# Encoder layer on one core: per-partition vectors by one transpose, one bias table of full width, one mask store per head and row half

## The chip, the cores and the metric

The kernel runs on one core of a Trainium2 chip. The metric is the device time of one execution in microseconds (us), lower is better. Times are medians over several executions; the profile is one execution, recorded by the hardware profiler, with times counted from the start of its span.

## The reference

One encoder layer is applied to two batches of 1024 tokens of width 1024, with the same weights, in f32. Cut to what matters here:

```
proj = x @ w_in                       # q, k, v of mixer A and B, and two gates
ya = mixer_a(...)                     # dilated sliding windows
# mixer B: 2-D neighbourhood attention, 8 heads, with a learned bias
bias = rpb[:, dr, dc]                 # rpb is (8 heads, 15, 31)
bias = where(ok, bias, -1e30)
scores = q k^T / 8 + bias
merged = sigmoid(ga + b_gate[0]) * ya + sigmoid(gb + b_gate[1]) * yb
x = layer_norm(alpha * x + merged @ w_out, ln1_g, ln1_b)
hid = square(relu(x @ w_ff1 + b_ff1))
x = layer_norm(alpha * x + hid @ w_ff2 + b_ff2, ln2_g, ln2_b)
```

The vectors `b_gate`, `ln1_g`, `ln1_b`, `b_ff1` (called `b1`) and `b_ff2` (`b2`) are used per feature. Where features lie on partitions, each is wanted as a column: entry k*128 + p on partition p.

## The kernel before

`encoder_kernel` handles the two batches one after the other (loop over `b`). f32 products are made of three reduced-precision products of high and low parts (`mm3`, lines 107 to 109), so every operand is split: ScalarE (ACT) casts the high part, VectorE (DVE) or GpSimd (POOL) subtracts it to get the low part (line 103 is the helper `sub` for all such subtractions).

**Start of a batch.** Eight tiles of x (`xt`, line 298) are loaded and transposed on TensorE into `xT`. Then comes the V stage: three groups of V columns, of 384, 384 and 512 columns. For each group `load_v` loads eight row blocks of weights into the ring `wvr` (tile name "wvr" of the pool `vrp`, four buffers, line 291), ACT casts and POOL subtracts them into `wv`. For each of eight token tiles TensorE makes 24 matmuls into a PSUM tile `psv` (four buffers); ACT casts it into `vt` (two buffers, line 342), DVE subtracts the low part, and ACT's own DMA queue stores `vt` into the DRAM tensor `vd` (line 344). 192 matmuls make a group. After the V stage come the first projections of mixer A (`pmm`, two PSUM buffers, 24 matmuls each), read by ACT on line 451 (`r`), shuffled by DVE and multiplied on POOL (lines 453 and 454) by the rotary table `rope`, which is loaded into memory that the V stage gives back (line 355).

**Tables, in the first batch only.** `bias_tables` (from line 139) pads the learned bias to `rp`, stores it to DRAM (`prd`, line 147) and copies it DRAM to DRAM into three tables `ud`, one for each of three column types of width 24, 32 and 24 (line 153): 184 x 16 rows each, so that the bias of a query row is read as one long run. Then the vectors are loaded as columns: `bg`, `gb1`, `agb`, `b1t` (lines 311 to 320), every element an address of its own, and two combined vectors go back to DRAM as `agd` the same way (line 319). `mask_tables` (from line 156) makes, for each type, head and row half (3 x 8 x 2 = 48 units), the masked bias: load `bt` from `ud` (line 168, six buffers), add the mask `maskb` on POOL (line 171), store to `bmd` (line 172). Mixer B reads `bmd` much later (line 654).

**What sets the order.** The tile framework schedules the program: within an engine the instructions stand in a fixed order, found when the program is built. Loads and table stores stand in SP's queue in one order with the weights; `vd` stores stand in ACT's. A DMA signals its landing on one of eight counters, DMAHW0 to DMAHW7, which SP's and ACT's DMAs share: a DMA that is given a counter waits, in its queue, until the DMA before it on this counter has landed.

Of the kernel before, what the change touches and what calls it, by code (L numbers as in the profile page):

```python
# [9 lines left out]
F32 = mybir.dt.float32  # L10
F32R = mybir.dt.float32r
AF = mybir.ActivationFunctionType
ALU = mybir.AluOpType
# [5 lines left out]
P = 128  # L19
T = 1024  # L20
D = 1024
KT = D // P
FF = 4096
ALPHA = 2.0 ** 0.25
# [7 lines left out]
TYPE_W = (24, 32, 24)  # L32
TYPE_DC = (23, 15, 15)
NROW = 12
MOFF = (0, 288, 672, 960, 1248, 1632)
# [46 lines left out]
def encoder_kernel(ctx, tc, xs, w_in, b_gate, w_a, w_b, w_out, rpb, ln1_g, ln1_b, w1, b1, w2, b2,  # L82
# [3 lines left out]
    def pool(name, bufs=1, side=None, space=None):  # L86
        kw = {} if space is None else {"space": space}
        if space is not DRAM:
            kw["reuse_waits"] = "tile"
        if side is not None:  # L90
            kw["side"] = side
        return tc.alloc_tile_pool(name=name, bufs=bufs, **kw)
# [19 lines left out]
    const = ctx.enter_context(tc.tile_pool(name="const", bufs=1))  # L112
    ident = const.tile([P, P], F32, name="ident")
    nc.sync.dma_start(ident, ident_d)
    bg = const.tile([P, 2, KT], F32, name="bg")
    gb1 = const.tile([P, 2, KT], F32, name="gb1")
    b1t = const.tile([P, FF // P], F32, name="b1t")
    mhalf = const.tile([P, 1], F32, name="mhalf")
    nc.gpsimd.memset(mhalf, -0.5)
    lnc = const.tile([P, 3], F32, name="lnc")  # L120
# [11 lines left out]
    agd = dram.tile([2, D], F32, name="agd")  # L132
    rawd = [dram.tile([4, P, 2, 4, P], F32, name=f"rawd{b}") for b in range(len(xs))]
    prd = dram.tile([8, PR, PC], F32, name="prd")
    ud = [dram.tile([16, 8 * PR, TYPE_W[ty]], F32, name=f"ud{ty}") for ty in range(3)]

    bmd = [dram.tile([8, 2, P, NROW * TYPE_W[ty]], F32, name=f"bmd{ty}") for ty in range(3)]

    def bias_tables():

        bp = pool("biasprep", side="right")
        rp = bp.tile([8, PR, PC], F32, name="rp")
        nc.gpsimd.memset(rp, 0.0)
        rq = bp.tile([8, 15, 31], F32, name="rq")
        nc.sync.dma_start(rq, rpb)
        nc.gpsimd.tensor_copy(rp[:, 4:19, 8:39], rq)
        nc.sync.dma_start(prd, rp)
        bp.release()
        prh = prd[:]
        for ty in range(3):  # L150
            w = TYPE_W[ty]
            src = bass.AP(tensor=prh.tensor, offset=prh.offset + TYPE_DC[ty], ap=[[PC, 8 * PR], [-1, 16], [1, w]])
            nc.sync.dma_start(ud[ty].rearrange("q r c -> r q c"), src)

    def mask_tables():

        mbp = pool("maskb", side="right")
        maskb = mbp.tile([P, 1920], F32, name="maskb")
        nc.sync.dma_start(maskb, maskb_d)
        btp = pool("btm", 6, side="right")  # L160
        for ty in range(3):
            w = TYPE_W[ty]
            n = NROW * w
            u = ud[ty][:]
            for h in range(8):
                for rh in range(2):
                    t = btp.tile([P, 384], F32, name="bt", tag="bt")
                    nc.sync.dma_start(t[:, :n], bass.AP(tensor=u.tensor, offset=u.offset + (h * PR + 4 - 4 * rh) * w,
                                                        ap=[[w, 8], [8 * PR * w, 16], [1, n]]))
                    mo = MOFF[3 * rh + ty]  # L170
                    nc.gpsimd.tensor_tensor(t[:, :n], t[:, :n], maskb[:, mo:mo + n], op=ALU.add)
                    nc.sync.dma_start(bmd[ty][h, rh], t[:, :n])
        btp.release()
        mbp.release()

# [91 lines left out]
    for b, x in enumerate(xs):  # L267
# [40 lines left out]
        if b == 0:  # L308
            with tc.issue_after(ins.ins):
                bias_tables()  # L310
                nc.sync.dma_start(bg, b_gate.rearrange("s (k p) -> p s k", p=P))
                for i, v in enumerate((ln1_g, ln1_b)):
                    nc.sync.dma_start(gb1[:, i], v.rearrange("(k p) -> p k", p=P))
                agb = const.tile([P, 3, KT], F32, name="agb")
                nc.sync.dma_start(agb[:, 2], b2.rearrange("(k p) -> p k", p=P))
                nc.vector.tensor_scalar(agb[:, 0], gb1[:, 0], ALPHA, None, op0=ALU.mult)
                nc.vector.tensor_scalar(agb[:, 1], gb1[:, 1], ALPHA, None, op0=ALU.mult)
                nc.vector.tensor_tensor(agb[:, 1], agb[:, 1], agb[:, 2], op=ALU.add)
                nc.sync.dma_start(agd.rearrange("s (k p) -> p s k", p=P), agb[:, :2])
                nc.sync.dma_start(b1t, b1.rearrange("(k p) -> p k", p=P))  # L320
        vz = vtp.tile([64, 256], F32, name="vz", tag="vt")
        nc.gpsimd.memset(vz, 0.0)
        for q in range(2):
# [288 lines left out]
        for hp in range(4):  # L612
# [19 lines left out]
            for c2 in range(2):  # L632
# [8 lines left out]
                for hd in range(2):  # L641
                    d0 = slice(64 * hd, 64 * hd + 64)
                    po = pspo.tile([P, 2, 2, P], F32, name="po", tag="po")
                    for ci in range(2):
                        cb = 2 * c2 + ci
                        ty = CB_TYPE[cb]
                        w, c0 = TYPE_W[ty], CB_C0[cb]
                        n, kn = NROW * w, 4 * w
                        pth = pp.tile([P, 4, 2, P], F32R, name="pth", tag="pth")
                        ptl = pp.tile([P, 4, 2, P], F32R, name="ptl", tag="ptl")  # L650
                        for rh in range(2):
                            if (ty, hd, rh) not in bt:
                                t = btp.tile([P, 384], F32, name="bt", tag="bt")
                                nc.sync.dma_start(t[:, :n], bmd[ty][2 * hp + hd, rh])
                                bt[ty, hd, rh] = t
                            S = pss.tile([P, 384], F32, name="S", tag="S")
                            us = slice(512 * rh + P * cb, 512 * rh + P * (cb + 1))
                            Sv = S[:, :n].rearrange("p (r c) -> p r c", c=w)
                            kv_ = [t[:, 4 * rh:4 * rh + NROW, c0:c0 + w] for t in kv]
                            nc.tensor.matmul(Sv, qs[hd][:, us], kv_[hd], start=True, stop=False)  # L660
                            nc.tensor.matmul(Sv, qs[hd][:, us], kv_[2 + hd], start=False, stop=True)
                            st2 = sm.tile([P, 2], F32, name="st2", tag="st2")
                            pr = head_unit(S, n, bt[ty, hd, rh], (st2[:, 0:1], st2[:, 1:2]), True, 0, n)
                            pt = pspt.tile([P, 3, P], F32, name="pt", tag="pt")
# [449 lines left out]
```

## Time and profile before

| | before |
|---|---|
| median of 3 runs | 3175.51 us (3169.77 to 3178.15) |
| profiled execution | 3184.45 us |
| its span | 3182.6 us |
| TensorE (PE) busy | 2951.2 us, 93% |
| VectorE / ScalarE / GpSimd busy | 1881.0 / 1449.7 / 979.1 us |
| mean granted TensorE clock | 0.959 of full speed |

The span leaves out 1.85 us of the profiled execution. A window row gives, for a stretch of the span, each engine's busy us and number of instructions, the granted TensorE clock (1.00 is full speed, 2.4 GHz; 0.50 is 1.2 GHz; between them lies a mixture), the mean busy share of the 16 DMA engines and their rate. A timeline row gives the start, the duration, the engine and the instruction, and in brackets how long the engine had been idle before it and what ended that. "SPq" and "ACTq" rows are DMA issues; their duration is that of the issue, not of the transfer.

### The profile page before, as it was taken

Reading aid. Unit: us, or ns where it says so; the run is one execution under the profiler, and the core shown is the slowest. Engines: PE = TensorE matmul, PEld = TensorE weight load, DVE = VectorE, ACT = ScalarE, POOL = GpSimd, SP = SyncE. Lnnn points to the kernel's source line nnn. Section 1 sums busy time; section 2 is a strip of 40 time slices with the busy share of each in tenths; the row PEclk is TensorE's granted clock in tenths of the full one; section 3 lists DMA queues with packets and bytes.
Section 4 is the critical chain, followed back from the end, with each engine's and each line's share of the span. In section 5 each row is a group of like instructions: output and inputs, shape, how many; then the busy total and the mean of one; then the engine's idle time right before and its main releaser. Section 6 shows DMA issues by size and latency. Waiting matters only on the chain. (4 is left out here: it accounts for less than half of the span.)

```text
span 3182.6 us, 39432 instructions
## 1 busy us (share of the span) xinstructions
PE 2951.2 (93%) x13964; PEld 2441.7 (77%) x13964; DVE 1881.0 (59%) x3439; ACT 1449.7 (46%) x2640; POOL 979.1 (31%) x716
## 2 busy tenths in 40 slices
PE   7879898999997899899989998989999979998997
PEld 7757786888786788688878786878877767886886
DVE  1036566673465666687861565567444756558887
ACT  3136564554363455333441564646542735553333
POOL 3464563223203200133341655432130131004322
PEclk9989898999998999899999999989999989999998
DMA  8742224345546644654354123244454575466442
GB/s 182 255 130 81 74 71 119 119 131 189 174 143 189 201 159 159 237 177 155 96 195 141 56 79 90 66 135 121 158 157 151 169 226 191 146 210 208 148 139 86
DMA packets 404414, 470.22 MB, mean 148 GB/s; under 512 B 44841, under 2 KB 282225, under 8 KB 403961
## 3 DMA queue, kind: packets, MB, share of 16 engines
q1 hardware_dynamic: 377720, 429.43, 43.1%
q10 hardware_dynamic: 26496, 38.28, 3.6%
q8 instruction: 110, 1.80, 0.2%
q14 instruction: 88, 0.71, 0.1%
HBM read 326.77 MB, written 141.79 MB: 147 GB/s over the span
## 5 line engine op out<-in xcount | busy, mean ns | idle before, releaser
L107 PE MATMUL pmm<-bh,whi 128*128 128x512 f32 x1152 | 465.4, 404 | 29.5 <-ACT r L451 23.6
L108 PE MATMUL pmm<-bh,wlo 128*128 128x512 f32 x1152 | 463.2, 402 | 0.0
L109 PE MATMUL pmm<-bl,whi 128*128 128x512 f32 x1152 | 462.7, 402 | 0.0
L103 POOL TENSOR_TENSOR wlo<-wraw,whi 128x512 fp32r<-128x512 f32 (+1 forms) x176 | 231.8, 1331 | 533.0 <-ACT whi L195 493.1
L107 PEld LDWEIGHTS pmm<-bh,whi 128*128 128x128 f32 x1152 | 221.1, 192 | 72.8 <-ACT r L451 24.9
L109 PEld LDWEIGHTS pmm<-bl,whi 128*128 128x128 f32 x1152 | 220.9, 192 | 42.7
L108 PEld LDWEIGHTS pmm<-bh,wlo 128*128 128x128 f32 x1152 | 221.0, 192 | 40.3
L103 POOL TENSOR_TENSOR ts<-rw,rw 128x1024 f32<-128x1024 f32 x14 | 41.4, 2957 | 655.7 <-DMA rw<-in_w_ff_dram 497.4
L746 ACT CAST bh<-hr 128x1024 fp32r<-128x1024 f32 x56 | 58.7, 1048 | 366.0 <-PE px L109 216.9
L391 ACT ACTIVATE smk<-smk,nm 128x256 f32<-128x256 f32 (+4 forms) x320 | 162.0, 508 | 129.1 <-DVE nm L390 126.1
L103 DVE TENSOR_TENSOR ptl<-pt,pth 128x512 fp32r<-128x512 f32 (+3 forms) x224 | 125.3, 569 | 67.4 <-ACT pth L667 36.7
L107 PE MATMUL psv<-wv,bh 128*128 128x384 f32 (+1 forms) x384 | 139.7, 365 | 19.8 <-DVE vt L103 18.2
L103 DVE TENSOR_TENSOR vt<-psv,vt 128x384 fp32r<-128x384 f32 (+1 forms) x48 | 28.8, 602 | 214.4 <-ACT vt L342 214.4
L108 PE MATMUL psv<-wv,bl 128*128 128x384 f32 (+1 forms) x384 | 139.9, 364 | 0.3 <-DVE bl L103 0.3
L109 PE MATMUL psv<-wv,bh 128*128 128x384 f32 (+1 forms) x384 | 138.5, 363 | 1.6 <-POOL wv L103 1.5
L107 PE MATMUL px<-bh,oh 128*128 128x512 f32 x256 | 106.4, 416 | 32.4 <-ACT oh L746 25.3
L103 POOL TENSOR_TENSOR qs<-r,qs 64x512 fp32r<-64x512 f32 x80 | 116.8, 1460 | 63.2 <-ACT qs L414 58.9
L108 PE MATMUL px<-bh,ol 128*128 128x512 f32 x256 | 105.6, 413 | 20.1 <-DVE ol L103 20.1
L746 ACT CAST oh<-ss 128x1024 fp32r<-128x1024 f32 x64 | 66.9, 1053 | 123.9 <-DVE ss L103 93.7
L103 DVE TENSOR_TENSOR bh<-hr,bh 128x1024 fp32r<-128x1024 f32 x56 | 84.0, 1500 | 57.5 <-ACT bh L746 57.4
L107 PE MATMUL pso<-woh,bh 128*128 128x512 f32 x256 | 103.9, 406 | 11.8 <-DVE sg L720 11.8
L960 POOL TENSOR_TENSOR rr<-rr,rg 128x512 f32<-128x512 f32 x32 | 48.7, 1542 | 212.1 <-DMA rr<-resd 199.0
(283 smaller groups left out, 8480.7 us busy)
## 6 DMA issues: line engine op xcount, KB each, us to landing
hr<-hidd SPq DMA_DIRECT2D x112, 512.0 KB
hidd<-ht SPq DMA_DIRECT2D x192, 256.0 KB
wraw<-in_w_in_dram SPq DMA_DIRECT2D x144, 256.0 KB
rw<-in_w_ff_dram SPq DMA_DIRECT2D x64, 512.0 KB
w1t<-in_w_ff_dram SPq DMA_DIRECT2D x40, 512.0 KB
gd<-gt ACTq DMA_DIRECT2D x32, 512.0 KB
sg<-gd SPq DMA_DIRECT2D x32, 512.0 KB
w1b<-in_w_ff_dram SPq DMA_DIRECT2D x32, 512.0 KB
```

The costliest lines, as they stand in the source:

```text
L103: eng.tensor_tensor(out, a, b, op=ALU.subtract)
L107: nc.tensor.matmul(out, ah, bh, start=start, stop=False, skip_group_check=skip)
L108: nc.tensor.matmul(out, al, bh, start=False, stop=False, skip_group_check=skip)
L109: nc.tensor.matmul(out, ah, bl, start=False, stop=stop, skip_group_check=skip)
L391: nc.scalar.activation(pr[:, e0:e1], pr[:, e0:e1], AF.Exp, bias=nm, scale=1.0, accum_out=den)
L746: nc.scalar.copy(oh, src)
L960: nc.gpsimd.tensor_tensor(rt[:, j], rt[:, j], gt[:, 0], op=ALU.mult)
```

## The change

1. One tile `par` (128 x 64) takes the place of `bg`, `gb1` and `b1t`. The four vectors are loaded as 64 contiguous rows of 128 values into `prm`, a buffer of the ring `wvr`; one transpose on TensorE and one copy on DVE make `par`.
2. `agb` is now 8 rows of three vectors of 128 values, in a second buffer of the ring `wvr`; the three small operations and the store `agd` are the same, in contiguous rows.
3. There is one table `ud`, of width 32, and one `bmd` of 960 columns. `mask_tables` has 16 units (head, row half): one load `bt` (192 KB, three buffers), three additions on POOL that read slices of it, into `bo` (two buffers), one store (480 KB).
4. Mixer B reads a slice of `bmd`.

```diff
-    bg = const.tile([P, 2, KT], F32, name="bg")
-    gb1 = const.tile([P, 2, KT], F32, name="gb1")
-    b1t = const.tile([P, FF // P], F32, name="b1t")
+    par = const.tile([P, 64], F32, name="par")
+    bg, gb1 = (par[:, 16 * i:16 * i + 16].rearrange("p (s k) -> p s k", s=2) for i in range(2))
+    b1t = par[:, 32:64]
...
-    ud = [dram.tile([16, 8 * PR, TYPE_W[ty]], F32, name=f"ud{ty}") for ty in range(3)]
-    bmd = [dram.tile([8, 2, P, NROW * TYPE_W[ty]], F32, name=f"bmd{ty}") for ty in range(3)]
+    ud = dram.tile([16, 8 * PR, TYPE_W[1]], F32, name="ud")
+    bmd = dram.tile([8, 2, P, MOFF[3]], F32, name="bmd")
...
-        for ty in range(3):
-            w = TYPE_W[ty]
-            src = bass.AP(tensor=prh.tensor, offset=prh.offset + TYPE_DC[ty], ap=[[PC, 8 * PR], [-1, 16], [1, w]])
-            nc.sync.dma_start(ud[ty].rearrange("q r c -> r q c"), src)
+        src = bass.AP(tensor=prh.tensor, offset=prh.offset + TYPE_DC[1], ap=[[PC, 8 * PR], [-1, 16], [1, TYPE_W[1]]])
+        nc.sync.dma_start(ud.rearrange("q r c -> r q c"), src)
...
-        btp = pool("btm", 6, side="right")
-        for ty in range(3):
...
-            for h in range(8):
-                for rh in range(2):
-                    t = btp.tile([P, 384], F32, name="bt", tag="bt")
-                    nc.sync.dma_start(t[:, :n], bass.AP(tensor=u.tensor, offset=u.offset + (h * PR + 4 - 4 * rh) * w,
-                                                        ap=[[w, 8], [8 * PR * w, 16], [1, n]]))
-                    mo = MOFF[3 * rh + ty]
-                    nc.gpsimd.tensor_tensor(t[:, :n], t[:, :n], maskb[:, mo:mo + n], op=ALU.add)
-                    nc.sync.dma_start(bmd[ty][h, rh], t[:, :n])
+        btp = pool("btm", 3, side="right")
+        bop = pool("bom", 2, side="right")
...
+                t = btp.tile([P, NROW, w1_], F32, name="bt", tag="bt")
+                nc.sync.dma_start(t, bass.AP(tensor=u.tensor, offset=u.offset + (h * PR + 4 - 4 * rh) * w1_,
+                                             ap=[[w1_, 8], [8 * PR * w1_, 16], [1, NROW * w1_]]))
+                o = bop.tile([P, MOFF[3]], F32, name="bo", tag="bo")
+                for ty in range(3):
...
+                    nc.gpsimd.tensor_tensor(ov, t[:, :, c0:c0 + w], mv, op=ALU.add)
+                nc.sync.dma_start(bmd[h, rh], o)
...
-                nc.sync.dma_start(bg, b_gate.rearrange("s (k p) -> p s k", p=P))
-                for i, v in enumerate((ln1_g, ln1_b)):
-                    nc.sync.dma_start(gb1[:, i], v.rearrange("(k p) -> p k", p=P))
-                agb = const.tile([P, 3, KT], F32, name="agb")
-                nc.sync.dma_start(agb[:, 2], b2.rearrange("(k p) -> p k", p=P))
...
-                nc.sync.dma_start(agd.rearrange("s (k p) -> p s k", p=P), agb[:, :2])
-                nc.sync.dma_start(b1t, b1.rearrange("(k p) -> p k", p=P))
+                prm = vrp.tile([P, 512], F32, name="prm", tag="wvr")[:64, :P]
+                for i, v in enumerate((b_gate.rearrange("s (k p) -> (s k) p", p=P), ln1_g.rearrange("(k p) -> k p", p=P),
+                                       ln1_b.rearrange("(k p) -> k p", p=P), b1.rearrange("(k p) -> k p", p=P))):
+                    r0 = (0, 16, 24, 32)[i]
+                    nc.sync.dma_start(prm[r0:r0 + v.shape[0]], v)
+                ppt = pst.tile([P, 4, P], F32, name="pt", tag="pt")
+                nc.tensor.transpose(ppt[:, 0, :64], prm, ident[:64, :64])
+                nc.vector.tensor_copy(par, ppt[:, 0, :64])
+                agb = vrp.tile([P, 512], F32, name="agb", tag="wvr")[:KT].rearrange("k (s p) -> k s p", p=P)
+                for i, v in enumerate((ln1_g, ln1_b, b2)):
+                    nc.sync.dma_start(agb[:, i], v.rearrange("(k p) -> k p", p=P))
...
+                nc.sync.dma_start(agd.rearrange("s (k p) -> k s p", p=P), agb[:, :2])
...
-                                nc.sync.dma_start(t[:, :n], bmd[ty][2 * hp + hd, rh])
+                                nc.sync.dma_start(t[:, :n], bmd[2 * hp + hd, rh][:, MOFF[ty]:MOFF[ty] + n])
```

SP's queue, first batch, after the last load of x: before.

```order
L311 DMA bg<-in_b_gate_dram 128x16x1
L313 DMA gb_61<-in_ln_g_dram 128x8x1
L313 DMA gb_61<-in_ln_b_dram 128x8x1
L315 DMA agb<-in_b_ff_dram 128x8x1
L320 DMA b1t<-in_b_ff_dram 128x32x1
L291 DMA wvr<-in_w_in_dram 128x512
L319 DMA agd<-agb 128x16x1
L147 DMA prd<-rp 8x1081
L153 DMA ud_89<-prd 184x16x24
L153 DMA ud_90<-prd 184x16x32
L153 DMA ud_91<-prd 184x16x24
L159 DMA maskb<-in_maskb_dram 128x1920
```

The same place in the changed program (its own line numbers).

```order
L318 DMA prm<-in_b_ff_dram 32x128
L324 DMA agb<-in_ln_g_dram 8x128
L324 DMA agb<-in_ln_b_dram 8x128
L324 DMA agb<-in_b_ff_dram 8x128
L146 DMA prd<-rp 8x1081
L293 DMA wvr<-in_w_in_dram 128x384 x2
L150 DMA ud<-prd 184x16x32
L328 DMA agd<-agb 8x2x128
L293 DMA wvr<-in_w_in_dram 128x384 x6
L156 DMA maskb<-in_maskb_dram 128x1920
L165 DMA bt<-ud 128x1x384 x3
```

The eight weight loads of the second V group (128x384), which stood between the loads of x before, now stand here, two ahead of `ud` and six behind `agd`, since `prm` and `agb` take two of the ring's four buffers ahead of them.

ACT's queue where the first V group ends and the second begins, with the counters that each waits for: before.

```order
L342 CAST vt<-psv 128x6x64 [waits PE_49]
L292 CAST wv_1023<-wvr 128x512 [waits DMAHW2_49]
L344 DMA vd_71<-vt 128x3x256 [waits DMAHW2_49,DVE_49]
L342 CAST vt<-psv 128x6x64 [waits DMAHW7_49,PE_49]
L292 CAST wv_1023<-wvr 128x512 [waits DMAHW1_49]
L344 DMA vd_71<-vt 128x3x256 [waits DMAHW6_49,DVE_49]
```

And in the changed program.

```order
L350 CAST vt<-psv 128x6x64 [waits DMAHW7_49,PE_49]
L352 DMA vd_69<-vt 128x3x256 [waits DMAHW5_49,DVE_49]
L350 CAST vt<-psv 128x6x64 [waits DMAHW6_49,PE_49]
L294 CAST wv_945<-wvr 128x512 [waits DMAHW2_49,Pool_49]
L352 DMA vd_69<-vt 128x3x256 [waits DMAHW7_49,DVE_49]
L294 CAST wv_945<-wvr 128x512 [waits DMAHW3_49]
```

Before, the first of these `vd` stores takes DMAHW2 after the first `bt` load, which stands behind all three `ud` copies and the mask load; now it takes DMAHW5 after the mask load, and the next DMAHW7 after the first `bt` load, behind one `ud` copy. Apart from this stretch the order of TensorE's matmuls in the first two stages is the same but for a few rows.

## Rows read from the trace of the kernel before

**Rows 1.** The page: the span, and TensorE's busy time, share and instructions.

```profile
span 3182.6 us, 39432 instructions
PE 2951.2 (93%) x13964; PEld 2441.7 (77%) x13964; DVE 1881.0 (59%) x3439; ACT 1449.7 (46%) x2640; POOL 979.1 (31%) x716
```

**Rows 2.** Timeline of TensorE: the four matmuls that began after a long wait.

```profile
87.34 0.69 PE L107 MATMUL psv<-wv,bh 128*128 128x384 f32 x1 [16.95 <-DVE vt L103]
...
94.57 0.44 PE L107 MATMUL psv<-wv,bh 128*128 128x384 f32 x1 [1.23 <-DVE vt L103]
...
177.25 0.79 PE L107 MATMUL pmm<-bh,whi 128*128 128x512 f32 x1 [14.19 <-ACT r L451]
...
198.41 0.79 PE L107 MATMUL pmm<-bh,whi 128*128 128x512 f32 x1 [7.25 <-ACT r L451]
```

**Rows 3.** Timeline of ACT: around 55 to 86 us, and the end of the V stage.

```profile
55.08 0.47 ACT L342 CAST vt<-psv 128x384 fp32r<-128x384 f32 x1
...
86.21 0.48 ACT L342 CAST vt<-psv 128x384 fp32r<-128x384 f32 x1 [30.15 <-DMA bt<-ud]
...
174.79 0.58 ACT L342 CAST vt<-psv 128x512 fp32r<-128x512 f32 x1 [5.49 <-DMA bmd<-bt]
176.13 0.37 ACTq L344 DMA_DIRECT2D vd<-vt  x1
```

**Rows 4.** Waits between 36 and 178 us: us in total, times, longest us.

```profile
ACT vt L342 <- DMA bt<-ud: 63.0, 6, 30.1
```

**Rows 5.** Timeline of SP's queue, 34 to 180 us: DMA issues.

```profile
34.02 0.33 SPq L298 DMA_DIRECT2D xt<-in_x_prompt_dram  x1
...
46.61 2.40 SPq L147 DMA_DIRECT2D prd<-rp  x1
59.58 13.02 SPq L153 DMA_DIRECT2D ud<-prd  x3
72.64 6.11 SPq L159 DMA_DIRECT2D maskb<-in_maskb_dram  x1
79.28 3.73 SPq L168 DMA_DIRECT2D bt<-ud  x6
...
170.91 5.39 SPq L172 DMA_DIRECT2D bmd<-bt  x5
...
178.94 0.42 SPq L355 DMA_DIRECT2D rope<-in_rope_dram  x1
```

**Rows 6.** Windows: PE, PEld, DVE, ACT, POOL busy (x), PEclk, DMA share, GB/s.

```profile
43.00:50.00 7.00, 6.42 (x40) 6.00 (x39) 2.87 (x7) 2.19 (x5) 0.00 (x0) 1.00 1.11 161
50.00:59.50 9.50, 9.50 (x56) 9.50 (x55) 0.85 (x2) 2.56 (x5) 3.79 (x3) 1.00 0.78 42
59.50:72.00 12.50, 10.89 (x62) 10.56 (x60) 0.00 (x0) 0.00 (x0) 0.00 (x0) 1.00 0.53 52
```

**Rows 7.** Windows as in rows 6, of other stretches.

```profile
60.00:70.00 10.00, 10.00 (x58) 10.00 (x57) 0.00 (x0) 0.00 (x0) 0.00 (x0) 1.00 0.59 57
...
87.30:100.00 12.70, 11.44 (x55) 11.12 (x56) 1.62 (x3) 3.82 (x7) 10.17 (x11) 0.86 0.90 290
...
177.20:198.40 21.20, 13.91 (x48) 10.85 (x48) 4.90 (x8) 4.59 (x9) 12.23 (x11) 0.74 0.54 176
```

**Rows 8.** The third V group alone (instructions on `psv`; columns without POOL).

```profile
126.00:146.00 20.00, 20.00 (x87) 16.00 (x87) 2.08 (x3) 2.24 (x4) 1.00 0.77 274
```

**Rows 9.** DMA packets, by size, from 36 to 86 us and from 86 to 177 us.

```profile
DMA packets 23277, 5.53 MB, mean 111 GB/s; under 512 B 20405, under 2 KB 22798, under 8 KB 23273
...
DMA packets 20561, 23.25 MB, mean 255 GB/s; under 512 B 1412, under 2 KB 20044, under 8 KB 20556
```

**Rows 10.** Timeline of POOL: one addition of each size, and the wait for the rotary table.

```profile
126.12 1.01 POOL L171 TENSOR_TENSOR bt<-bt,maskb 128x384 f32<-128x384 f32 x1 [2.08 <-DMA bt<-ud]
...
175.16 0.79 POOL L171 TENSOR_TENSOR bt<-bt,maskb 128x288 f32<-128x288 f32 x1 [0.41 <-DMA bt<-ud]
...
186.80 1.29 POOL L453 TENSOR_TENSOR r<-r,rope 128x512 f32<-128x512 f32 x1 [8.74 <-DMA rope<-in_rope_dram]
```

More of the change, by code (lines that the diff above doesn't have):

```diff
@@ L159, in mask_tables @@
         nc.sync.dma_start(maskb, maskb_d)
-        btp = pool("btm", 6, side="right")
-        for ty in range(3):
-            w = TYPE_W[ty]
-            n = NROW * w
-            u = ud[ty][:]
-            for h in range(8):
-                for rh in range(2):
-                    t = btp.tile([P, 384], F32, name="bt", tag="bt")
-                    nc.sync.dma_start(t[:, :n], bass.AP(tensor=u.tensor, offset=u.offset + (h * PR + 4 - 4 * rh) * w,
-                                                        ap=[[w, 8], [8 * PR * w, 16], [1, n]]))
-                    mo = MOFF[3 * rh + ty]
-                    nc.gpsimd.tensor_tensor(t[:, :n], t[:, :n], maskb[:, mo:mo + n], op=ALU.add)
-                    nc.sync.dma_start(bmd[ty][h, rh], t[:, :n])
+        btp = pool("btm", 3, side="right")
+        bop = pool("bom", 2, side="right")
+        w1_ = TYPE_W[1]
+        u = ud[:]
+        for h in range(8):
+            for rh in range(2):
+                t = btp.tile([P, NROW, w1_], F32, name="bt", tag="bt")
[3 more added lines that the diff above has]
+                for ty in range(3):
+                    w, c0 = TYPE_W[ty], TYPE_DC[ty] - TYPE_DC[1]
+                    ov, mv = (v.rearrange("p (r c) -> p r c", c=w) for v in
+                              (o[:, MOFF[ty]:MOFF[ty] + NROW * w], maskb[:, MOFF[3 * rh + ty]:MOFF[3 * rh + ty] + NROW * w]))
+                    nc.gpsimd.tensor_tensor(ov, t[:, :, c0:c0 + w], mv, op=ALU.add)
+                nc.sync.dma_start(bmd[h, rh], o)
+        bop.release()
         btp.release()
@@ L310, in encoder_kernel @@
                 bias_tables()
-                nc.sync.dma_start(bg, b_gate.rearrange("s (k p) -> p s k", p=P))
-                for i, v in enumerate((ln1_g, ln1_b)):
-                    nc.sync.dma_start(gb1[:, i], v.rearrange("(k p) -> p k", p=P))
-                agb = const.tile([P, 3, KT], F32, name="agb")
-                nc.sync.dma_start(agb[:, 2], b2.rearrange("(k p) -> p k", p=P))
-                nc.vector.tensor_scalar(agb[:, 0], gb1[:, 0], ALPHA, None, op0=ALU.mult)
-                nc.vector.tensor_scalar(agb[:, 1], gb1[:, 1], ALPHA, None, op0=ALU.mult)
+                prm = vrp.tile([P, 512], F32, name="prm", tag="wvr")[:64, :P]
[9 more added lines that the diff above has]
+                    nc.sync.dma_start(agb[:, i], v.rearrange("(k p) -> k p", p=P))
+                for i in range(2):
+                    nc.vector.tensor_scalar(agb[:, i], agb[:, i], ALPHA, None, op0=ALU.mult)
                 nc.vector.tensor_tensor(agb[:, 1], agb[:, 1], agb[:, 2], op=ALU.add)
-                nc.sync.dma_start(agd.rearrange("s (k p) -> p s k", p=P), agb[:, :2])
-                nc.sync.dma_start(b1t, b1.rearrange("(k p) -> p k", p=P))
+                nc.sync.dma_start(agd.rearrange("s (k p) -> k s p", p=P), agb[:, :2])
         vz = vtp.tile([64, 256], F32, name="vz", tag="vt")
```

## The prediction

> **What bounds the kernel now.** I read the page first: TensorE is busy for 2951.2 of 3182.6 us [rows 1], so an edit away from TensorE moves the time only where TensorE waits for it, or runs at the lower clock after a wait. All that the change touches lies in the first 200 us of the first batch (later there is only another address for the reads of `bmd`). There TensorE waits four times at length: 16.95, 1.23, 14.19 and 7.25 us [rows 2], 39.6 us in all. The next views say what each hangs on.
>
> The first two: DVE waits for ACT's cast of `vt`, and ACT stood idle for 30.15 us before its cast at 86.21 us, until a `bt` load landed [rows 3, 4]. ACT needs no bias there; its `vd` store in between had been given the counter of the first `bt` load. That load stood in SP's queue behind all the table work: `prd` at 46.61, `ud` from 59.58, the mask from 72.64, `bt` from 79.28 us [rows 5]. TensorE went on until its four `psv` tiles were full, which is at 87.34 - 16.95 = 70.4 us.
>
> The third: the V stage's last casts wait in the same way for mask loads and stores (63.0 us of ACT's waits end with a `bt` load [rows 4]; the last cast, at 174.79 us, with a `bmd` store [rows 3]). So the V stage ends with the mask units: the last `vd` store goes out at 176.13 us, the last `bmd` stores run from 170.91 to 176.30 us [rows 3, 5]. The fourth: only then is the rotary table loaded (178.94 us), POOL starts on it at 186.80 us [rows 5, 10], and TensorE goes on at 198.41 us [rows 2].
>
> **The change part by part.** TensorE's prices come first: 58 matmuls of 384 columns in 10.00 us at full clock [rows 7] are 0.172 us each, 4.14 us per V tile of 24; 87 of 512 columns in 20.00 us [rows 8] are 0.230 us each, 5.52 us per tile.
>
> *The small transfers.* Gone are the columns of single values: 2048 + 1024 + 1024 + 1024 + 4096 loaded and 2048 stored, 11,264 packets, and two `ud` copies of 184 x 16 = 2944 packets. With the copy that stays that is 20,096 of the 20,405 packets under 512 B in 36 to 86 us [rows 9]. They cost no bandwidth but time: from 50 to 59.5 us the DMA engines are 0.78 busy for 42 GB/s [rows 6], and `prd` (34 KB) needs from 49.0 to 59.58 us until `ud` may go [rows 5]. The three copies and the mask load behind them hold the queue from 59.58 to 79.28 us, at most 6.6 us per copy; the new copy is of the middle size.
>
> *The new start.* The last load of x waits for TensorE, so it stays at 34.02 us [rows 5]. Seven small loads of contiguous rows at about 0.4 us per issue (as for x and the rotary table [rows 5]), and a wait for that last x tile among them, bring SP to about 39.5 us for `prd`; it lands after an estimated 2.5 us, as there is nothing slow ahead of it. Then `ud` (42 to 49), `agd` (to about 51), six weight loads, the mask at 56, the first `bt` at 57, landed at about 61 us. The `vd` store that waits for it goes 9 us before TensorE would have to stop. So both first waits go, and with them the half clock behind them: 55 matmuls took 11.44 us at a clock of 0.86 [rows 7] against 55 x 0.172 = 9.46, 2.0 us. Term: -(16.95 + 1.23 + 2.0) = **-20.2 us**.
>
> *What it costs there.* The weights of the second V group were loaded among the x tiles; now two of the eight come before `ud` and six behind `agd`. TensorE reaches this group at 70.4 - 4 x 4.14 = 53.8 us. By the times above the third to eighth block land between 50 and 57 us, and each needs ACT's cast and a POOL subtraction of about 1.0 us (as the 384 wide addition [rows 10]). The last is usable at 58.5 us; TensorE wants it at 57.4. Nothing hides this: queued behind it are TensorE's whole second group, and the POOL subtractions that free the ring. From below it is 0; from above, with `prd` as slow as before (10.6 instead of 2.5 us) and `ud` taking the 13.02 us that all three issues took [rows 5], 15 us more, so 16 to 18. I take **+4 us**, near the low end, since the slow packets ahead are gone. The transpose is one matmul among 192; with the DVE copy and a slightly other order of DVE's small operations I put +0.5 us, hidden by nothing on TensorE but by its tiles in flight on DVE.
>
> *The mask units.* POOL's work stays: 32 additions at 0.79 and 16 at 1.01 us [rows 10], 41.4 us, 2.6 us per unit of the new form (whether reading slices of `bt` costs more no row shows; half as much again would add 1.3 us per unit). The loads fall from 7.7 to 3.1 MB, the stores stay at 7.9 MB in 16 instead of 48. The chain starts at about 61 us instead of 79.28. Its earliest end is POOL's: 61 + 41.4 + eight weight subtractions of about 1.29 us (as the 512 wide product [rows 10]) = 113 us. By bytes: 11 MB of mask units, 8 of `vd`, 3 of weights and mask, 22 MB; at the 255 GB/s of 86 to 177 us [rows 9] that is 86 us, end 147; at full share (274 / 0.77 = 356 GB/s [rows 8]) 62 us, end 123. Before, SP's queue also waited for POOL and had 23% of the DMA time unused, so I take 135, between. TensorE by itself ends the V stage at 53.8 + 8 x 4.14 + 8 x 5.52 + 4 = 135 us. So the two meet, and the third wait goes, with its half clock: 48 matmuls took 13.91 us [rows 7] against 48 x 0.230 = 11.0, 2.9 us. Term: -(14.19 + 2.9) = **-17.1 us**; from above, with an end at 147, 12 us less.
>
> A bound on the `vd` stores: a `bmd` row is now 3840 bytes, a `vd` row 1024. If the two queues took turns row by row, `vd` would get a fifth of the 356 GB/s, 75 GB/s, and a 512 KB store would take 7.0 us against TensorE's 5.52 per tile: 12 us more over eight tiles while `bmd` is backed up. The Trainium skill ("DMA: Bandwidth & Descriptors", section "Queues, rings and completion order") has the engines change queues at the boundary of a packet that gathers several descriptors; by that both would get about half, and these 12 us would be nothing. No row here shows which; I leave the 12 us in the range.
>
> *The rotary table.* From the last `vd` store to TensorE's return took 198.41 - 176.13 = 22.3 us. Before, TensorE had already done two of its four `pmm` tiles when it stopped; now all four, 22.1 us, lie beside that chain. The fourth wait shrinks to about 3 us: **-4 us** (from 0 to -7.25).
>
> Mixer B's reads move the same bytes in the same number of loads: nothing. Sum: -20.2 + 4 + 0.5 - 17.1 - 4 = -36.8, rounded to -36.5 us. Check: TensorE's return at 198.41 becomes 161.9, against 135 + 22 to 25 = 157 to 160. The rest of the program is a fixed order behind that point and moves as a whole: the span becomes 3146 us. The profiled execution (3184.45) is 9 us over the median of 3175.51, so I subtract from the median: **3139 us**.
>
> **The rivals.**
> *The chain keeps its pace.* Before, 480 KB of masks were stored per (176.3 - 79.3) / 16 = 6.1 us. If the stores set that pace and not the number of operations, or the `vd` stores are held back as above, the chain ends at 61 + 97 = 158 us, and the V stage with it: 18 us earlier than 176. Time 3157. For it: ACT's waits on counters stay, and there are now two buffers to store from. Against: POOL and the loads took part in the 97 us.
> *The change does not do what it says.* If `prd` and `ud` are slow by themselves (34 KB over eight rows; rows of 128 bytes), the mask chain starts at 79 as before and keeps its pace: the V stage ends at 176, and the wait for weights replaces the first stall. Time 3175.
> *Slower: the weights behind the tables.* If the stretch from `prd` to `bt` takes its old 79.28 - 46.61 = 32.7 us, the six blocks land from 72 us on: TensorE waits from 55 to about 77, 22 us in place of 17, and the chain starts at 82. With two buffers and a store that takes as long as two old stores, 6.6 us per unit, it ends at 187 us, 11 us later than now: 3187. It decides from about 30 us for the stretch together with 6.4 us per unit. Against it: the slow packets that filled that stretch are the ones removed.
>
> **How the numbers follow.** Forecast, 3124 to 3150: 0.62. The chain keeps its pace, 3150 to 3163: 0.22. No effect: 0.08. Slower: 0.08. A measurement tells a difference of 0.3%, 9.5 us, from none, so faster is 0.62 + 0.22 = 0.84, same 0.08, slower 0.08. The range takes the forecast with its bounds and the first rival: 3123 (all four waits gone, no new one, and some half clock more: -52) to 3162.
>
> **What would show it.** Right: the `ud` copy goes out before 45 us and lands within 8; TensorE has no wait over 5 us between 50 and 130; the last `bmd` store lies before 145 and the last `vd` store near 135; after 165 the program is the old one, 35 us earlier. Wrong: TensorE waits for `wv` at 54 us for more than 8 us (my +4 term); ACT's casts still wait for `bt` or `bmd` after 100 us (the chain); or the later stages differ by more than 5 us, which would mean that the order found for them matters.

## The result, and the profile of the changed kernel

| | before | changed |
|---|---|---|
| median, us | 3176.83 | 3142.24 |
| lowest to highest, us | 3169.77 to 3180.42 | 3135.0 to 3147.21 |
| ratio, with 95% interval | 1 | 0.9887 (0.9869 to 0.9904) |
| span of the profiled execution, us | 3182.6 | 3143.0 |

By the ratio the changed kernel is faster by 36 us (30 to 42); 36.5 us were forecast. That the sum came out so close is luck: the trace shows 47 us saved in the first 200 us, and some 10 us lost again behind them, by something that the prediction did not have at all. The page of the changed kernel begins so (it answers to [rows 1]):

```profile
span 3143.0 us, 39310 instructions
PE 2959.1 (94%) x13965; PEld 2432.1 (77%) x13965; DVE 1881.8 (60%) x3440; ACT 1452.1 (46%) x2640; POOL 976.5 (31%) x716
DMA packets 378373, 464.94 MB, mean 148 GB/s; under 512 B 26889, under 2 KB 254137, under 8 KB 377921
```

The span fell by 39.6 us, and the four waits of [rows 2] were 39.6 us long, which tempts one to stop here. But TensorE's busy time has grown, from 2951.2 to 2959.1 us, although half clock after three of the waits has gone as well. Both numbers come back below.

The longest of TensorE's waits in the first 260 us are now these; four others are of 0.2 or 0.3 us (line and what it waits for, us in total, times, longest):

```profile
PE pt L213 <- DMA xt<-in_x_prompt_dram: 6.1, 2, 5.4
PE po L387 <- DVE ptl L103: 0.4, 1, 0.4
PE S L510 <- DVE kk L425: 0.3, 1, 0.3
```

So all four waits of [rows 2] are gone, the one for the rotary table too. SP's queue (start, duration, what it issues), which answers to [rows 5]:

```profile
37.66 0.27 SPq L146 DMA_DIRECT2D prd<-rp  x1
...
39.57 0.77 SPq L150 DMA_DIRECT2D ud<-prd  x1
40.44 5.80 SPq L328 DMA_DIRECT2D agd<-agb  x1
46.34 6.30 SPq L293 DMA_DIRECT2D wvr<-in_w_in_dram  x6
52.68 0.42 SPq L156 DMA_DIRECT2D maskb<-in_maskb_dram  x1
53.16 2.50 SPq L165 DMA_DIRECT2D bt<-ud  x3
...
114.84 6.87 SPq L173 DMA_DIRECT2D bmd<-bo  x3
...
131.05 0.35 SPq L363 DMA_DIRECT2D rope<-in_rope_dram  x1
```

`ud` goes 1.9 us behind `prd` (before: 13.0), the first `bt` at 53.16 instead of 79.28 us, and the rotary table at 131.05 instead of 178.94 us, before the last `vd` store. POOL's first mask additions, its last, and its first step on the rotary table:

```profile
61.95 5.02 POOL L172 TENSOR_TENSOR bo<-bt,maskb 128x288 f32<-128x288 f32 x6 [4.28 <-DMA bt<-ud]
...
118.82 2.54 POOL L172 TENSOR_TENSOR bo<-bt,maskb 128x288 f32<-128x288 f32 x3 [0.93 <-DMA bmd<-bo]
...
139.57 1.29 POOL L461 TENSOR_TENSOR r<-r,rope 128x512 f32<-128x512 f32 x1 [7.78 <-DVE r L460]
```

The chain of mask units runs from 61.95 to 121.4 us, 59 us. In the kernel before it began at 85.81 us, and with the addition at 175.16 us [rows 10] it ended at 175.95, so it took 90 us. What POOL's additions waited for is in the next rows; first the kernel before (its first additions, and all between 55 and 180 us), then the changed one between 55 and 125 us (busy time, mean ns, idle time just before and what ended it):

```profile
85.81 1.54 POOL L171 TENSOR_TENSOR bt<-bt,maskb 128x288 f32<-128x288 f32 x2 [27.81 <-DMA bt<-ud]
...
L171 POOL TENSOR_TENSOR bt<-bt,maskb 128x288 f32<-128x288 f32 (+1 forms) x48 | 41.5, 871 | 69.8 <-DMA bt<-ud 52.2 <-issue 10.0 <-POOL bt L171 3.3
```

```profile
L172 POOL TENSOR_TENSOR bo<-bt,maskb 128x288 f32<-128x288 f32 (+1 forms) x48 | 40.5, 878 | 13.3 <-DMA bmd<-bo 6.7 <-DMA bt<-ud 4.3 <-issue 1.5
```

Before, 52.2 of 69.8 us of idle time ended with a `bt` load; 27.8 of them are the wait ahead of the first addition, so 24.4 lie within the chain. Now 4.3 us do, all of them ahead of the first addition. Reading a slice of the wide table costs 878 instead of 871 ns on the mean, nothing. ACT's casts (start, duration, idle before and what ended it) follow TensorE in the third V group, where in [rows 3] the last followed a mask store. Between 60 and 86 us some still wait for a `vd` store, the longest 6.23 us, but TensorE does not stop for it:

```profile
63.20 0.48 ACT L350 CAST vt<-psv 128x384 fp32r<-128x384 f32 x1 [6.23 <-DMA vd<-vt]
...
103.78 0.59 ACT L350 CAST vt<-psv 128x512 fp32r<-128x512 f32 x1 [5.01 <-DMA vd<-vt]
...
120.58 0.59 ACT L350 CAST vt<-psv 128x512 fp32r<-128x512 f32 x1 [5.01 <-PE psv L109]
...
131.78 0.59 ACT L350 CAST vt<-psv 128x512 fp32r<-128x512 f32 x1 [5.01 <-PE psv L109]
133.12 0.37 ACTq L352 DMA_DIRECT2D vd<-vt  x1
137.21 0.60 ACT L459 ACTIVATE r<-pmm 128x512 f32<-128x512 f32 x1 [4.84 <-PE pmm L109]
```

Last, TensorE by stretches of the changed kernel (length, busy time, products, granted clock, share of the DMA engines, GB/s):

```profile
50.00:59.50 9.50, 9.10 (x48) 1.00 0.78 244
60.00:70.00 10.00, 10.00 (x60) 1.00 0.96 309
...
87.30:100.00 12.70, 12.70 (x56) 1.00 0.89 309
...
120.00:140.00 20.00, 20.00 (x88) 1.00 0.71 234
```

From 60 us on TensorE is busy throughout at a clock of 1.00, where [rows 7] had 0.86 and 0.74. Only from 50 to 59.5 us something is missing: 48 products instead of some 55, the new wait for weights.

Matching product by product (the changed program has one more, the transpose; the order is nearly the same), the lead of the changed kernel over the kernel before is 20.1 us at the 400th product, 37.2 at the 700th, 47.0 at the 800th and still 47.1 at 310 us. Then it shrinks: 42.4 us at the 4800th, 44.7 at the 7000th, 39.6 at the end. Seven to eight of the early 47 us are lost in stages that the change does not touch. The experiments had to find out both what made the early gain and what took this back.

### The profile page after: what moved, and what is told of

It reads as the page before. It is cut to its first block, busy times and chain, and to the rows that moved or that the text cites. A ratio compares the mean times of both kernels' runs of the same rounds, so it can differ in the third digit from the quotient of the medians.

```text
span 3143.0 us, 39310 instructions
## 1 busy us (share of the span) xinstructions
PE 2959.1 (94%) x13965; PEld 2432.1 (77%) x13965; DVE 1881.8 (60%) x3440; ACT 1452.1 (46%) x2640; POOL 976.5 (31%) x716
## 5 line engine op out<-in xcount | busy, mean ns | idle before, releaser
L108 PE MATMUL px<-bh,ol 128*128 128x512 f32 x256 | 106.8, 417 | 21.1 <-DVE ol L103 21.1
```

Of the source, the lines that this page charges most:

```text
L108: nc.tensor.matmul(out, al, bh, start=False, stop=False, skip_group_check=skip)
```

## Experiments

All ratios below are to the kernel before, run beside on the same chip; 0.1% is 3.2 us. Where two kernels ran on different chips, their difference is that of their ratios. The first four take the change apart.

**The vectors alone.** The kernel before, with the rows, the transpose and `par`; the tables stay.

```diff
-    bg = const.tile([P, 2, KT], F32, name="bg")
-    gb1 = const.tile([P, 2, KT], F32, name="gb1")
-    b1t = const.tile([P, FF // P], F32, name="b1t")
+    par = const.tile([P, 64], F32, name="par")
...
+                nc.tensor.transpose(ppt[:, 0, :64], prm, ident[:64, :64])
+                nc.vector.tensor_copy(par, ppt[:, 0, :64])
```

> The kernel before with the vectors' part alone: rows instead of columns and the transpose; the three ud copies, 48 mask units and their stores as before. My theory (the small packets cost queue time at the start, the mask chain's length is a matter of the units): prd goes out near 39.5 us and lands within 3 us, the three ud copies still take 13 us, so the second V group's weights come behind them (TensorE waits for wv 8 to 15 us near 55 us), the first bt goes out near 72 us instead of 79.28, and the chain takes its old 97 us, so the V stage ends near 169 instead of 176: 7 to 12 us under before. Rival (what counts is the number of packets under 512 B, of which the vectors are about two thirds of those removed): two thirds of the 35 us, 24 us under before, with the chain much shorter than 97 us.

Measured: 3180.93 us, ratio 1.0001 (0.9991 to 1.0011). Neither theory had said that the time would stay. In its SP queue the start is as expected:

```profile
37.97 0.27 SPq L147 DMA_DIRECT2D prd<-rp  x1
...
39.85 14.03 SPq L153 DMA_DIRECT2D ud<-prd  x3
53.98 5.89 SPq L326 DMA_DIRECT2D agd<-agb  x1
59.98 6.95 SPq L291 DMA_DIRECT2D wvr<-in_w_in_dram  x6
```

and so is TensorE's new wait (waits up to 260 us):

```profile
PE pmm L107 <- ACT r L457: 21.4, 2, 11.3
PE psv L107 <- ACT wv L292: 11.4, 2, 11.1
```

The six blocks of weights stand behind three `ud` copies and cost 11.1 us. The chain of 48 units runs from 75.67 to 169.3 us, 94 us, no faster than before. At 310 us this kernel is 8.3 us ahead of before, as expected; at the end it is 0.4 us behind. It has lost 9 us on the way, much like the changed kernel with its 7 to 8.

**The tables alone.** The changed kernel with the column-wise loads and stores of before.

```diff
-    par = const.tile([P, 64], F32, name="par")
+    bg = const.tile([P, 2, KT], F32, name="bg")
...
-                nc.sync.dma_start(agd.rearrange("s (k p) -> k s p", p=P), agb[:, :2])
+                nc.sync.dma_start(agd.rearrange("s (k p) -> p s k", p=P), agb[:, :2])
```

> The changed kernel with the old column-wise loads of the vectors and the column-wise store of agd: one ud copy, 16 units with one load and one store. My theory: prd lands as late as before (ud from 59 to 60 us), one copy instead of three saves 13 us of the queue less little, the first bt goes out at 66 to 67 us, a first wait of TensorE of 5 to 9 us stays, no new wait for weights, the chain takes 59 us as in the changed kernel and ends near 127, so the third and fourth waits go: 28 to 36 us under before. Rival (number of packets under 512 B): one third of the 35 us, 12 us under before, with the chain or the start still slow.

Measured: 3143.62 us, ratio 0.9882 (0.9866 to 0.9898): all the gain of the whole change. TensorE's waits up to 260 us have the small rest of the first stall, and nothing else of length:

```profile
PE psv L107 <- DVE vt L103: 6.3, 2, 4.5
PE pt L213 <- DMA xt<-in_x_prompt_dram: 5.6, 1, 5.6
```

At 310 us it is 37.6 us ahead, 9 us less than the changed kernel; but it loses nothing later, and ends 45.0 us ahead, where the changed kernel ends 39.6 us ahead. (All leads are to one profiled execution of before, so the difference between two of them says more than one alone.) The vectors' part therefore does bring 9 us at the start, and the same part costs about as much later.

**The rows of `agd` alone.** The kernel before, with one of its column-wise transfers made contiguous. It copies `ln1_g` and `ln1_b` straight into `agd`, and so leaves out the scaling by alpha and the addition of `b2`.

```diff
-                nc.sync.dma_start(agd.rearrange("s (k p) -> p s k", p=P), agb[:, :2])
+                for i, v in enumerate((ln1_g, ln1_b)):
+                    nc.sync.dma_start(agd[i].rearrange("(k p) -> k p", p=P), v.rearrange("(k p) -> k p", p=P))
```

> The kernel before with agd written as contiguous rows straight from ln1_g and ln1_b (left out: the scaling by ALPHA and the addition of b2, so the residual of the first norm is another); the column-wise loads, three ud copies and 48 units stay. This asks what made prd land 10.6 us after its issue and held the DMA engines 0.78 busy at 42 GB/s from 50 to 59.5 us: the 2048 stores of one value each, or the 9216 loads of one value each. If the stores: prd lands within 4 us, ud goes out near 52 us, the mask chain starts 7 to 9 us earlier, 7 to 10 us under before. If the loads (my guess, by their number): ud still goes out within 2 us of 59.58, and the time is within 3 us of before.

Measured: 3170.48 us, ratio 0.9966 (0.9954 to 0.9978), 10.8 us less. The guess was wrong: the stores alone are worth this. Its SP queue:

```profile
35.39 0.40 SPq L311 DMA_DIRECT2D bg<-in_b_gate_dram  x1
...
42.59 0.58 SPq L321 DMA_DIRECT2D b1t<-in_b_ff_dram  x1
43.28 3.18 SPq L291 DMA_DIRECT2D wvr<-in_w_in_dram  x1
46.56 0.31 SPq L147 DMA_DIRECT2D prd<-rp  x1
49.34 13.20 SPq L153 DMA_DIRECT2D ud<-prd  x3
```

With all 9216 loads of one value still there, `ud` goes 2.8 us behind `prd`; with the 2048 stores of one value it went 13.0 us behind [rows 5]. So 8 KB of stores held the queue up by 10 us. The loads cost time at another place, ahead of `prd`: here it is issued at 46.56 us, 11.2 us after the first column load and as late as in the kernel before (46.61 us), where with rows it is issued at 37.66 us (changed) and 37.97 us (vectors only). Of the 20 us by which `ud` goes earlier in the changed kernel (39.57 for 59.58 us) the stores thus account for about 10, and 9 lie ahead of `prd`, where the columns became rows and the weights of the second group moved. The stores stood right before `prd`, the loads 4 us and more before it; the loads were not tried in the stores' place.

**The vectors in a pool of their own.** The changed kernel, so that the second V group's weights are loaded among the x tiles again.

```diff
-                prm = vrp.tile([P, 512], F32, name="prm", tag="wvr")[:64, :P]
+                vecp = pool("vec", side="right")
+                prm = vecp.tile([P, P], F32, name="prm")[:64]
```

> The changed kernel with the rows of the vectors in a pool of their own instead of two blocks of the weights' ring, so that the weights of the second V group are loaded early again, among the x tiles. My theory (the new wait for weights is about 1.2 us, since 48 matmuls lie where 55 lay from 50 to 59.5 us): the dip at 50 to 59.5 us goes, and the time is 0 to 3 us under the changed kernel. Rival (weights loaded early stand ahead of prd and delay the tables, and the first vd store waits again for a bt load): a wait of TensorE near 70 us comes back, and the time is 0 to 8 us over the changed kernel.

Measured: 3131.21 us, ratio 0.9845 (0.9826 to 0.9865), 13 us under the changed kernel. At 310 us it leads that kernel by 0.9 us only, what the theory gave to the wait for weights. The rest comes later and is taken up again below.

**Addresses.** What the changed kernel and the vectors-only kernel share, and the tables-only kernel does not, is that the 96 bytes per partition of `agb` are gone from the const pool. Every tile of the pools above it starts 96 bytes lower (`bh` at 17,344 instead of 17,440), while the tiles on the right side, the weights' halves among them, stay. (These addresses are those of the built programs; the traces do not show them.) In the traces the products themselves had changed. In 90 us of `px`, `py` and `pz` without a wait, at full clock, before:

```profile
1181.00:1271.00 90.00, 90.00 (x395) 1.00 0.47 150
```

and changed, in the same stage:

```profile
1138.00:1228.00 90.00, 90.00 (x387) 1.00 0.47 149
```

Eight products fewer, with nothing to wait for. The theory: the price of a product hangs on the distance between the addresses of its two operands. Four kernels with an unused tile in the const pool, and not one instruction in another place, try it.

```diff
+    const.tile([P, 24], F32, name="pad")
     mhalf = const.tile([P, 1], F32, name="mhalf")
```

The changed kernel with 24 values (96 bytes), which restores the addresses of before:

> The changed kernel with an unused tile of 96 bytes per partition in the const pool, so that every later tile of the lower pools stands at the address it had before the change (the change takes the 96 bytes of agb out of that pool). My theory: the TensorE product's price depends on the distance, modulo 128 bytes, between the addresses of its two operands in a partition; the change moved pmm, pz and parts of px and py from distance 64 to 96, and the records show 233.1 instead of 229.7 ns for one of 512 columns. Then pmm goes back from 233.0 to 229.7 ns, px to 227.9, and the time is 8 to 16 us under the changed kernel (22 us by the records, less what lies under waits), near 0.984 of before. Rival (what the changed kernel and the vectors-only kernel lose after the first 300 us is scatter of the granted clock): prices of the products as in the changed kernel, time within 4 us of it.

Measured: 3127.75 us, ratio 0.9855 (0.9837 to 0.9872), 10 us under the changed kernel, and the products are back:

```profile
1126.00:1216.00 90.00, 90.00 (x395) 1.00 0.47 151
```

The kernel before with 8 values, which gives it the changed kernel's distances modulo 128:

> The kernel before with nothing but an unused tile of 32 bytes per partition in the const pool: the operands of pmm, pz, half of px and half of py at distance 96 modulo 128 bytes, as in the changed kernel, and nothing else of the change. My theory: pmm from 229.7 to 233.0 ns, and 8 to 14 us over before. Rival (what is lost after the first 300 us has to do with the change itself or with scatter): pmm stays at 229.7 ns, and the time is within 4 us of before.

Measured: 3184.49 us, ratio 1.0041 (1.0028 to 1.0055): 13 us lost by an unused tile of 32 bytes.

```profile
1177.00:1267.00 90.00, 90.00 (x387) 1.00 0.46 148
```

The kernel before with 16 values, and the own-pool kernel with 8, both meant to have distance 0:

> The kernel before with nothing but an unused tile of 64 bytes per partition in the const pool: all products of 512 columns have their operands at distance 0 modulo 128 bytes (before: 64 for pmm, psv, pz, half of px and half of py). My theory: pmm from 229.7 to 227, psv from 233.3 to 227 ns, 18 us by the records, and 8 to 16 us under before. Rival (addresses do not matter): within 4 us of before.

> The kernel with the vectors in their own pool, with an unused tile of 32 bytes per partition in the const pool: all products of 512 columns then have their two operands at distance 0 modulo 128 bytes. My theory (distance sets the price): pmm from 233.0 to 227, pz, py, px and psv to 226.5 to 227.5 ns, 40 us by the records over the whole run, of which half or more shows: 20 to 30 us under the own-pool kernel, so 3100 to 3112 us. Rival (addresses do not matter, the tiles' prices differ for another reason): within 4 us of the own-pool kernel.

Measured: 3180.26 us, ratio 1.0027 (1.0017 to 1.0036), for the kernel before with 64 bytes: 8.5 us lost where 8 to 16 were to be gained. The own-pool kernel with 32 bytes: 3108.75 us, ratio 0.9798 (0.9778 to 0.9817), 15 us under the own-pool kernel, less than the 20 to 30 expected, and the best of all. Their rows, first the one that missed its forecast:

```profile
1175.00:1265.00 90.00, 90.00 (x388) 1.00 0.46 150
```

```profile
1124.00:1214.00 90.00, 90.00 (x399) 1.00 0.46 145
```

One of two "zero" distances is cheap and one is dear, so the modulus was wrong. Sorted modulo 256 all traces agree. Addresses are again those of the built programs. This table is worked out from the starts of all products of 512 columns in the fourteen traces (mean time from one start to the next, those between 215 and 245 ns, so at full clock and without a wait); the distance is the moving operand's address less the stationary one's:

| distance mod 256 | ns | products | which |
|---|---|---|---|
| 0 | 227.1 | 67,026 | `pr`, `pso`, `pt`, half of `px`, part of `py` everywhere; all kinds in the two kernels with 399 |
| 32 | 233.3 | 2,304 | `psv`, changed and others with its const pool |
| 64 | 229.4 | 22,966 | `pmm`, `pz`, half of `px`, most of `py`, before and others with its const pool |
| 96 | 233.3 | 5,737 | the same, before with 32 bytes |
| 128 | 232.5 | 6,134 | the same and `psv`, before with 64 bytes |
| 160 | 234.2 | 384 | `psv`, before with 32 bytes |
| 192 | 233.3 | 1,534 | `psv`, before and others with its const pool |
| 224 | 233.1 | 34,595 | the same, changed and others with its const pool |

Products whose operands lie on the same side move together and keep their 227 ns in every kernel, so it is the distance and not the address. The tiles move under DVE and ACT too, but their busy times stay within 0.4% (DVE 1881.8 us changed, 1883.9 with 96 bytes, 1878.6 with 32). The changed kernel with 32 bytes, and the changed kernel once more beside it, put the refined rule to a test:

> The changed kernel with an unused tile of 32 bytes per partition: all products of 512 columns then have their operands at distance 0 modulo 256 bytes (the kernel before with 64 bytes had 128, and 232.4 ns instead of the 227 expected, so the rule goes by 256). My theory: pmm near 228.6, psv 226.9, px, py and pz near 227 ns; 40 us by the records, of which something like a half shows as from 229.7 to 233.1: 18 to 25 us under the changed kernel, 0.980 to 0.982 of before. Rival (products at less than 229 ns are taken back by the granted clock): not below the kernel with 96 bytes, 0.9855.

> The changed kernel once more, as the measure for the runs beside it on the same chip. My theory (its early stages always save 47 us, and its products always cost 233 ns at their distance): 0.987 to 0.990 of before, the same prices. Rival (its first result was luck of the granted clock): outside that.

Measured: 3121.41 us, ratio 0.983 (0.9817 to 0.9843), against 3142.35 us, ratio 0.989 (0.9877 to 0.9904): 21 us by an unused tile of 32 bytes, within the 18 to 25 expected. The stretch of `px` with it:

```profile
1125.00:1215.00 90.00, 90.00 (x399) 1.00 0.48 153
```

The records alone would give 34 us, not the 40 of the expectation (`pmm` 3456 x 4.3 ns, `px` 1536 x 6.4, `py` 816 x 6.4, `pz` 336 x 6.1, `psv` 384 x 6.4). In all five comparisons some half of what the records give shows in the time (10 of 22 us with 96 bytes, 13 of 24 and 8.5 of 18 on the kernel before, 21 of 34 here, 15 of 34 on the own-pool kernel). Where the other half goes, into longer waits for DVE and ACT or into the granted clock, was not followed.

**The own pool once more.**

> The kernel with the vectors in their own pool once more, beside the changed kernel. It has the same distances between operands, and its early part was 1.1 us shorter, yet it was 13 us faster over two sets of runs. My theory (the early part is the only real difference): 1 to 4 us under the changed kernel of this same call. Rival (something later is really faster): 9 to 15 us under it again.

Measured: 3126.73 us, ratio 0.9845 (0.9831 to 0.9858), 15.6 us under the changed kernel run beside it: the rival, something later is really faster. The two programs' orders differ, most of all in the feed-forward stages (from about the 4540th product on, and from the 11,400th in the second batch), where with the own pool the scheduler put products, casts and loads in another order. The lead over the changed kernel's repetition grows there: from -0.6 us at the 4500th product to 5.5 at the 5900th, and from 9.7 at the 11,390th to 17.6 at the 12,900th; between these it grows by 4 us, and at the end it is 17.4. In the second of these stages TensorE's largest waits are, in the changed kernel's repetition (2430 to 2860 us):

```profile
PE px L107 <- ACT oh L754: 12.1, 2, 10.8
PE px L108 <- DVE ol L103: 10.6, 3, 6.1
PE pt L107 <- ACT bh L754: 8.2, 1, 8.2
```

and in the own-pool kernel's (2421 to 2839 us):

```profile
PE px L107 <- ACT oh L756: 9.3, 1, 9.3
PE px L108 <- DVE ol L103: 6.3, 3, 4.5
...
PE pt L107 <- ACT bh L756: 4.1, 1, 4.1
```

31 us of waits in all instead of 38 (the two stretches are not cut at quite the same products: 1647 and 1663). So 14 of the 17.4 us of lead arise where the order is another, and it waits less there; what the order alone is worth, and why the scheduler chose it, is not shown. Early weights themselves are worth about 1 us.

**Three stores per mask unit.**

```diff
-                nc.sync.dma_start(bmd[h, rh], o)
+                for ty in range(3):
+                    m0, m1 = MOFF[ty], MOFF[ty] + NROW * TYPE_W[ty]
+                    nc.sync.dma_start(bmd[h, rh][:, m0:m1], o[:, m0:m1])
```

> The changed kernel with three stores of a third of a row per mask unit instead of one (48 in all, the same bytes). Which part of the unit set the old pace of 6.1 us per 480 KB? If the number of stores and their issues: the chain of 16 units grows from 59 us towards 97 and ends after 140 us. If the loads and the single buffer per type (my guess), or the bytes: it ends within 8 us of 121. The total changes by less than 6 us as long as the chain ends before 133.

Measured: 3139.56 us in one run, and in POOL's rows the first and the last units are

```profile
60.15 5.01 POOL L172 TENSOR_TENSOR bo<-bt,maskb 128x288 f32<-128x288 f32 x6 [3.00 <-DMA bt<-ud]
...
116.25 2.53 POOL L172 TENSOR_TENSOR bo<-bt,maskb 128x288 f32<-128x288 f32 x3 [0.96 <-DMA bmd<-bo]
```

58.6 us from start to end with 48 stores, 59.4 with 16. The number of stores alone did not set the old pace. The loads are what is left, and 24.4 us of POOL's idle time within the old chain ended with one; but this is argued. Whether it was their number (48 or 16), their bytes (7.9 or 3.1 MB) or their place in the queue behind stores that wait for POOL was not tried.

## Why the prediction was right, point by point

**The first two waits, -20.2, and the new cost, +4.5.** Together -15.7; the lead at the 400th product is 20.1 us. The waits went as described: `prd`, `ud`, mask and first `bt` came within 4 us of the times forecast (37.66, 39.57, 52.68 and 53.16 us for about 39.5, 42, 56 and 57). The term for the weights was too large. Its measure is the missing 7 products of 50 to 59.5 us, 1.2 us, and the 0.9 us that the own pool returns (the +0.5 for the transpose was not measured by itself); the blocks were loaded from 46.34 us on, 4 us before I had them. The slower rival's mechanism is real all the same: with three `ud` copies in front it took 11.1 us in the vectors-only kernel.

**The small transfers.** Right that they hold the queue. Not known then: of the 20 us by which `ud` goes earlier, about 10 go to the 2048 stores, behind which `prd` was slow; the loads stood in the 9 us ahead of `prd`.

**The mask units.** The chain ended at 121.4 us, inside the bounds of 113 and 147 and ahead of the 135 taken, so TensorE alone set the end of the V stage: last `vd` store 133.12, forecast 135. The first rival, that the chain keeps its pace, is out: 59 us for 90. Its own sum set the old chain at 97 us, counted from the issue of the first load (79.28 us), and added that to a start counted from the landing; by POOL's rows it would have ended near 151 and not at 158 us. The loads of the old chain were 7.9 MB like its stores, not 7.7; nothing hung on it. The 12 us for `vd` stores held back by longer `bmd` rows did not come: TensorE is busy without a gap from 60 us on, and of the eight casts of the third group seven end their idle time of about 5 us with a product and one with a `vd` store, in TensorE's step. What was drawn there from the Trainium skill ("DMA: Bandwidth & Descriptors", section "Queues, rings and completion order") is not tested by this: no row measures the queues' shares, and from a change of queue at the boundary of a packet it does not yet follow that both get half.

**The third and the fourth wait, -17.1 and -4.** Measured 26.9 us (from 20.1 to 47.0) for 21.1. The step that failed is the rotary table's. I let its chain of 22 to 25 us start behind the last `vd` store; but SP, done with the masks at 121.7 us, sent the load at 131.05, before that store, and the whole wait went. I had also forgotten half clock behind this wait. The kernel before has, from 198.4 to 215 us, 64 products at a clock of 0.85,

```profile
198.40:215.00 16.60, 16.59 (x64) 13.40 (x65) 9.44 (x17) 6.53 (x12) 10.97 (x9) 0.85 0.16 51
```

where 16.6 us at 0.23 us each would hold 72. That is 7.25 + 2 us instead of 4.

**"The rest of the program moves as a whole."** This step is wrong. Its own sign had been named, later stages that differ by more than 5 us, but for a different order. It is the addresses: with those of before the changed kernel is at 0.9855, 46 us faster, which is the early gain of 47; with its own it is at 0.9887. So the forecast of 36.5 us stands on two misses of about 10 us that cancel: the early gain was 47 and not 37, and the 96 bytes taken out of the const pool cost 10. The vectors-only kernel shows the same with the sum at zero: 8 us gained, 9 lost. With it falls the premise that all that the change touches lies in the first 200 us. The diff showed the cause (`agb` leaves `const`); TensorE's busy time on the page, up by 8 us, was its first trace.

## What to carry to other kernels

A product's price belongs among the things a change can move: when a small tile enters or leaves a pool at the bottom, compare how many products fit into the same busy stretch before and after, and try the distance of the operands (here multiples of 256 bytes were best) by an unused tile before anything else. A transfer that stores single values is worth removing for what stands behind it in the queue, not for its bytes. And when a total agrees with the forecast, check the terms at several points along the span; here each half was off by 10 us.

## What the runs showed of the hardware that I had not expected

- A TensorE product of 512 columns with fp32r operands takes 227.1 ns at full clock where the two operands' addresses in a partition differ by a multiple of 256 bytes, 229.4 at 64 more, and 232.5 to 234.2 at the other multiples of 32. What in the chip makes it so, no run here shows.
- 2048 stores of 4 bytes to DRAM, issued right before `prd`, delayed its landing by 10 us (`ud` 13.0 instead of 2.8 us behind `prd`). 9216 loads of 4 bytes, issued 4 us and more before it, did not; their issues, with one weight load behind them, took 11 us ahead of `prd` (35.39 to 46.56 us).
- POOL reads a slice of every wider row at the price of whole rows, 878 and 871 ns on the mean.
- 48 stores of a third of a row and 16 of a whole one took the same time, 58.6 and 59.4 us with all that lies between.
